# A diffusion block on one core: weight sums spread over another stretch, one sum moved to VectorE, modulation steps two slots earlier, four copies moved to ScalarE

## The chip, the cores and the metric

The kernel runs on one core of a Trainium2 chip. The metric is the device time of one execution in microseconds; the time before is the median of three runs. A trace is one profiled execution, and its times count from the span's start.

## The reference, cut to what matters

One layer works on 512 tokens of 1024 channels (float32), with 256 context tokens as a prefix. Its weights are read once from HBM.

```python
z = h @ w_in                                  # h: x, normed and modulated by c
u, vs, q, r, ga, gb, k, v, lr = split(z)
a  = spatial_gating(gelu(u), gelu(vs), ...)   # 128-token chunks
o  = gla_bidir(q, k, v, lr, ...)              # 4 heads, decays, two directions
ob = rms_norm(o) * gla_norm_g * silu(r)
merged = sigmoid(ga) * (a @ w_br_a) + sigmoid(gb) * (ob @ w_br_b)
x = x + g1 * (merged @ w_o)
x = x + g2 * conv_ffn(modulate(rms_norm(x), sh2, sc2))   # w_up, 3x3 conv, gelu, w_down
out = rms_norm(x)
# sh1, sc1, g1, sh2, sc2, g2 = split(silu(c) @ w_ada + b_ada)
```

## The kernel before, in words

Every product is made nearly exact in float32 by splitting both operands into a high and a low part (float32r) and adding three matmuls: high x high, high x low, low x high. TensorE (PE) does 4440 matmuls, most of them 128x128 by 512.

**The weight stream.** All weights but the very first come as a list of 190 loads of up to 512 KB (`specs`). `weights()` hands out the next one, splits one load further (`stream_split`) and issues loads up to four further (`stream_load`, L240, on SyncE's queue). A load fills one of five buffers `raw`; ScalarE casts it to the high part `wh` (L255), VectorE subtracts to get the low part `wl` (L256), and then the buffer is free for the load five places on. Loads are named here by their place in the list: 18 to 31 belong to r, 32 to 45 to vs, 46 to 59 to ga, 60 to 73 to gb, 74 to 87 to br_a. Loads 10 to 17 are the eight units of u.

**The gates.** r, vs, ga, gb and br_a are each a 1024-wide product of 512 tokens, made in seven products where eight quarters would be needed (`gate`, `gate_product`, a Strassen scheme). One product takes two loads and 24 matmuls into two PSUM banks (L1358). Some products go on accumulating in a bank whose earlier content has to be copied out first: r's fifth (s3) runs on in bank X, out of which ScalarE copies u2 (`taken`, L1341). The scheme needs sums and differences of quarters of the weight. They are built in DRAM ahead of time by GpSimd's DMA queue (POOL): plain copies (L221) and accumulating DMAs (L223), each 512 KB, in `sums_build`. A gate takes 16 of these (8 copies, 8 accumulating), or 12 (6 and 6) when it is one of the first `ADDED` gates: then the first sum is not built, the quarter itself is loaded, and VectorE adds to it the load two places before (`back`, L251). Held by that add, the older buffer comes free later.

**When the sums are issued.** `gate_sums` yields after every sum, and three callers take the next one. `weights()` takes one at each load before r, and from r on where `gate_pace` says so. `hook()`, called after the products of the first stages (each unit of u calls it twice), takes one more at every call from load 8 on. Some places in the first products take one directly. A sum is tied behind the last matmul issued before it (`behind_pe`).

**Heads.** The four heads of the linear attention run in `steps`, fed by `hook`, between the big products. `step_o` writes a head's output to four PSUM banks, two after two; each is copied to SBUF by VectorE (L1020), and ScalarE makes its sum of squares (L1022). Only then is the bank free; the next head's transposes (L953) take these banks.

**Modulation.** g1, sh2 and sc2 are computed on VectorE in small steps beside the gates (`ada2`): one step loads 256 KB of `w_ada` (L1184, SyncE) and does one multiply-add of 128x512 (L1188). A new group first fills its accumulators on ScalarE (L1174) and loads a row of `b_ada` into each (L1176, SyncE). `tick` takes one step; `ticks` is a list of how many steps are taken at each load of a gate.

**gb and the operand of br_a.** After gb's first product SyncE issues 16 loads of a kept operand (`aq<-kept`, L1501, in `a_prep`), which br_a will use. Where the code does not tie an order, a scheduler sets it for each engine.

Of the kernel before, what the change touches and what calls it, by code (L numbers as in the profile page):

```python
# [38 lines left out]
SHSC = 6  # L39
WT = (1, 1)  # L40
RAW = 5
ADDED = 3


@with_exitstack
def backbone_kernel(
# [7 lines left out]
    V, A, G, T = nc.vector, nc.scalar, nc.gpsimd, nc.tensor  # L54
# [19 lines left out]
    def late(shape, dt=F32, s="l"):  # L74
        return lp.tile(shape, dt, tag="l", name=nm(s))
# [7 lines left out]
    def gl():  # L83
        return pg.tile([P, 512], F32, tag="gl", name=nm("gl"))
# [81 lines left out]
    R_AT = len(specs)  # L166
# [14 lines left out]
    def w_block(ap, kn=2, back=0):  # L181
        specs.append((ap.rearrange("(k p) c -> p k c", p=P), kn, 512, back))
# [9 lines left out]
    for g, (g_quarter, g_sums) in enumerate(gate_weights):  # L192
        for n, f in enumerate((lambda b: g_quarter(b, 0, 0),
                               lambda b: g_quarter(b, 0, 1) if g < ADDED else g_sums[b][0], lambda b: g_sums[b][1],
                               lambda b: g_quarter(b, 1, 0), lambda b: g_sums[b][3], lambda b: g_quarter(b, 1, 1),
                               lambda b: g_sums[b][2])):
            for b in range(2):
                w_block(f(b), back=2 if n == 1 and g < ADDED else 0)
    down_specs[R_AT:R_AT] = specs
# [13 lines left out]
    def sums_build(quarter, sums, added=False):  # L213
        for step in ((((1, (0, 0)), (2, (1, 0)), (3, (0, 1))), ((3, (1, 1)),), ((1, 3),), ((2, 1),)) if added else
                     (((0, (0, 1)), (1, (1, 1)), (2, (1, 0)), (3, (0, 1))), ((0, (0, 0)), (3, (1, 1))),
                      ((1, 0),), ((2, 1),))):
            for b in range(len(sums)):
                for dst, src in step:
                    ap = quarter(b, *src) if isinstance(src, tuple) else sums[b][src]
                    if len(step) > 2:  # L220
                        behind_pe(lambda: G.dma_start(sums[b][dst], ap), G)  # L221
                    else:
                        behind_pe(lambda: G.dma_start(sums[b][dst], ap, accum_op=ALU.add), G)  # L223
                    yield

    def gate_sums():
        for g, z in enumerate(gate_weights):
            yield from sums_build(*z, g < ADDED)

# [3 lines left out]
    pos = [0, 0, 0]  # L233
# [37 lines left out]
        return lambda: V.tensor_tensor(wl, raw, wh.bitcast(F32), op=ALU.subtract)  # L271

    def gate_pace(i):
        return i % 3 if i > 45 else i % 4 == 0

    def weights():
        i = pos[2]
        pos[2] += 1
        for at, steps_ in building:
            for _ in range((i >= at and (at > 1 or i < R_AT or gate_pace(i))) + (at <= i < DENSE)):  # L280
                next(steps_, None)
        stream_split(i + 2)
        stream_load(i + 1 + AHEAD)
        return splits.pop(i)
# [648 lines left out]
    def mm3(ps, a, b, start, stop):  # L933
        for z, (p_, q_) in enumerate(((a[0], b[0]), (a[0], b[1]), (a[1], b[0]))):
            T.matmul(ps, p_, q_, start=(start and z == 0), stop=(stop and z == 2))  # L935
# [75 lines left out]
    def step_o(h, part):  # L1011
        S_ = heads[h]
        for i in ((1, 2), (0, 3))[part]:
            po = gl()
            oc = po[:, :256]
            for d in range(2):
                mm3(oc, [z[:, i * P:(i + 1) * P] for z in S_["qs"][d]], S_["st"][d][i], d == 0, False)
            mm3(oc, [z[:, i * P:(i + 1) * P] for z in S_["pt"]], S_["v"][i],
                False, True)
            V.tensor_copy(S_["o"][i // 2][:, i % 2, :], oc)  # L1020
            junk = late([P, 256], BF16, s="junk")
            A.activation(junk, oc, AF.Square, accum_out=oss[:, h, i:i + 1])  # L1022
        if part == 1:
            S_.clear()
# [3 lines left out]
    hooked = [0]  # L1028

    def hook():  # L1030
        hooked[0] += 1
        if (hooked[0] % 2 or pos[2] >= 8) and pos[2] < R_AT:
            next(building[1][1], None)
        if hooks:
            f = hooks.pop(0)
            f[0](*f[1:])
# [4 lines left out]
    def ctx_k(h, part):  # L1041
        ps = mm()
        for k in range(KT):
            wh, wl = part(k)
            ah, al = hc[k]
            for i, (a, b) in enumerate(((wh, ah), (wh, al), (wl, ah))):
                T.matmul(ps[:, :LC], a, b, start=(k == 0 and i == 0), stop=(k == KT - 1 and i == 2))  # L1047
        kcs[h] = heap([P, LC], s="kc")
        A.copy(kcs[h], ps[:, :LC])
        hook()  # L1050
# [5 lines left out]
    def x_unit(store, h):  # L1056
        w = weights()
        ps = mm()
        prod_cm(ps, w, hx)
        store[h] = heap([P, S], s="kq")  # L1060
        if store is qxs:
            A.mul(store[h], ps, QS)
        else:
            V.tensor_copy(store[h], ps)
        hook()
        return lambda k: [z[:, k, :] for z in w]

    def v_units():

        ws = [weights() for _ in range(KT // 2)]  # L1070
        v = []
        for t in range(6):
            ps = mm()
            for k in range(KT):
                wide_step(ps, ws[k // 2], hx if t < 4 else hc, t % 4, k)
            v.append(split_act(ps, s="v", lo_pool=late if t < 3 else heap, hi_pool=late, eng=A.copy))
            for h in (2, 3):
                heads[h].setdefault("v", []).append([z[:, (h - 2) * 256:(h - 1) * 256] for z in v[t]])
            hook()
            hook()  # L1080

    def steps(h):
        if h + 1 < NH:
            rest = [(step_u, h, 0, 3), (step_z, h + 1), (lambda: None,)]
        else:
            rest = [(step_u, h, n, n + 1) for n in range(3)]
        return [(step_transpose, h), (step_scores, h), (step_s0, h)] + rest + [(step_o, h, 0), (step_o, h, 1)]
# [275 lines left out]
    def gate(out, pool, at={}, mids=late, quad=r_quad, sum_=r_sum, pool1=None):  # L1363
        pool1 = pool1 or pool

        fresh = not banks
        banks.extend([bank() for _ in range(2)] for bank in (mm, gl, mm) if fresh)
        X, Z, Y = banks
        banks.reverse()
        later = lambda i: at.get(i, lambda: None)()  # L1370
        gate_product(X, quad("a11"), True)
        if fresh:
            m1 = [taken(z, mids) for z in X]
        else:
            for t in range(2):
                A.copy(Y[t], X[t])
        later(0)
        gate_product(Z, sum_("p1"), True)
        m5 = [taken(z, mids) for z in Z]
        later(1)  # L1380
        gate_product(X, sum_("s2"))
        u2 = [taken(z, mids) for z in X]
        later(2)
        gate_product(Y, quad("a21"), fresh)
        for t in range(2):
            out(0, t, combine(Y[t], m1[t], ALU.add, pool) if fresh else Y[t])
        later(3)
        gate_product(X, sum_("s3"))
        for t in range(2):
            out(1, t + 2, combine(m5[t], X[t], ALU.subtract, pool1))  # L1390
        later(4)
        gate_product(Z, sum_("q4"))
        for t in range(2):
            out(1, t, combine(Z[t], u2[t], ALU.subtract, pool1))
        later(5)
        gate_product(X, quad("a22"))
        later(6)
        for t in range(2):
            out(0, t + 2, X[t])
# [15 lines left out]
    def r_step(i):  # L1415
        if i == 2:
            piece()
        if i in (3, 5):
            sgu_load(i // 2 - 1)

    bg += [ada2("g1", ahead=5), ada2("sh", "sc", ahead=SHSC)]
    ticks = [0] * 4 + [1, 0] * 5 + [1, 0] * 7 + [0, 0] + [1] * 12 + [0, 1] * 7 + [1, 1, 2] * 5
    gate(r_out, heap, {i: lambda i=i: r_step(i) for i in range(7)}, heap)
    vraw = [[None] * 4 for _ in range(2)]
    stats = const([P, 4, 2, 6], "stats")
# [516 lines left out]
```

## Time and profile before

| what | value |
|---|---|
| time, three runs | 904.29 us median (903.58 to 906.23) |
| profiled execution, own time | 907.04 us |
| its span, first to last instruction | 905.3 us |
| mean granted TensorE clock | 0.996 |
| stage r (loads 18 to 31) | 246.2 to 288.6 us |
| stage vs (32 to 45) | 288.6 to 331.6 us |
| stage ga (46 to 59) | 331.6 to 377.9 us |
| stage gb (60 to 73) | 377.9 to 417.1 us |
| stage br_a (74 to 87) | 417.1 to 455.3 us |

A row of the profile gives engine, line, operation, and what was written from what (`wh<-raw`). A wait is put down to the one whose signal came last. The DMA share is the mean busy share of the core's 16 DMA engines; queue q0 is POOL's, q1 SyncE's, q10 ScalarE's. A share can stand a little over 1, since packets overlap. "Granted clock" is 1.00 when TensorE runs at full speed.

### The profile page before, as it was taken

The numbers are of one execution on the slowest core, as the hardware profiler recorded it, in microseconds if no ns is written. First come the engines' busy times: TensorE is split into PE (matmuls) and PEld (weight loads), VectorE is DVE, ScalarE is ACT, GpSimd is POOL, SyncE is SP. The second block draws the span as 40 slices with busy tenths as digits, with TensorE's granted clock in tenths as the row PEclk, the third lists the DMA queues.
The fourth block names the chain that finished last, engine by engine and source line by source line (L and its number), as shares of the span: only waits on it lengthen the run. The fifth ranks groups of instructions, "written<-read, shape, count | busy, mean of one in ns | idle before, by whom it ended". The sixth has DMA issues, their size and how long they took to land.

```text
span 905.3 us, 12519 instructions
## 1 busy us (share of the span) xinstructions
PE 888.0 (98%) x4440; PEld 739.6 (82%) x4440; DVE 733.9 (81%) x1223; ACT 481.4 (53%) x795; POOL 96.6 (11%) x150
## 2 busy tenths in 40 slices
PE   7999999999999999999999999999999999999996
PEld 5778888888877888888888889888888888888885
DVE  6478687969739889769998658897899987896996
ACT  6356465757636765577432348433343334356663
POOL 1302222222200000000000010001111110000000
PEclk9999999999999999999999999999999999999999
DMA  9976999999999977778995961998998893356552
GB/s 298 360 242 171 247 280 212 195 289 247 315 269 280 342 243 259 261 240 274 368 364 165 292 179 47 280 303 180 189 219 178 176 193 98 92 167 207 173 180 99
DMA packets 160268, 207.66 MB, mean 229 GB/s; under 512 B 9625, under 2 KB 88805, under 8 KB 160205
## 3 DMA queue, kind: packets, MB, share of 16 engines
q1 hardware_dynamic: 132861, 140.53, 48.6%
q0 software_dynamic: 24352, 61.04, 31.0%
q10 hardware_dynamic: 2992, 5.28, 1.5%
q8 instruction: 35, 0.57, 0.2%
q14 instruction: 28, 0.23, 0.1%
HBM read 198.43 MB, written 67.11 MB: 293 GB/s over the span
## 4 chain that ended last, share of the span: by engine, by line
PE 90%; DMA 4%; DVE 2%; ACT 2%; issue 0%; SPq 0%; ACTq 0%
PE mm L399 32%; PE mm L1358 13%; PE mm L417 10%; PE gl L1839 10%; PE gl L1358 5%; PE gl L935 2%; PE mm L699 2%; DMA fq<-fx 2%; DMA raw<-in_w_in_dram 2%; PE mm L1839 2%; PE gl L699 1%; PE mm L1047 1%; PE mm L1097 1%; PE gl L417 1%; PE gl L608 1%; PE gl L970 1%
## 5 line engine op out<-in xcount | busy, mean ns | idle before, releaser
L255 ACT CAST wh<-raw 128x1024 fp32r<-128x1024 f32 x189 | 194.8, 1036 | 189.3 <-PE mm L399 89.0
L256 DVE TENSOR_TENSOR wl<-raw,wh 128x1024 fp32r<-128x1024 f32 x189 | 226.1, 1203 | 61.8 <-ACT wh L255 60.2
L399 PE MATMUL mm<-h2h,wh 128*128 128x512 f32 (+1 forms) x344 | 133.0, 387 | 0.0
L399 PE MATMUL mm<-h2l,wh 128*128 128x512 f32 (+1 forms) x344 | 133.0, 387 | 0.0
L399 PE MATMUL mm<-h2h,wl 128*128 128x512 f32 (+1 forms) x344 | 133.0, 387 | 0.0
L1691 DVE SCALAR_TENSOR_TENSOR cacc<-ca,ccol,cacc 128x441 f32<-128x441 f32 (+2 forms) x176 | 121.9, 695 | 4.4
L399 PEld LDWEIGHTS mm<-h2h,wh 128*128 128x128 f32 x344 | 64.6, 188 | 13.1
L399 PEld LDWEIGHTS mm<-h2h,wl 128*128 128x128 f32 x344 | 64.6, 188 | 13.1
L399 PEld LDWEIGHTS mm<-h2l,wh 128*128 128x128 f32 x344 | 64.6, 188 | 13.0
L1839 PE MATMUL gl<-wh,dah 128*128 128x512 f32 x132 | 51.3, 389 | 0.0
L1839 PE MATMUL gl<-wl,dah 128*128 128x512 f32 x132 | 51.3, 389 | 0.0
L1839 PE MATMUL gl<-wh,dal 128*128 128x512 f32 x132 | 51.3, 389 | 0.0
L221 POOL DMA_DIRECT2D sum<-in_ffn_w_down_dram x24 | 13.2, 554 | 310.2 <-PE mm L417 196.1
L1188 DVE SCALAR_TENSOR_TENSOR acc<-wa,cs,acc 128x512 f32<-128x512 f32 x64 | 46.3, 749 | 0.0
L1692 ACT ACTIVATE cacc<-cacc 128x512 f32<-128x512 f32 x22 | 13.9, 633 | 59.4 <-DVE cacc L1691 59.4
L1358 PE MATMUL mm<-wh,xs 128*128 128x512 f32 x128 | 42.4, 402 | 2.7 <-ACT dt L1341 2.7
L223 POOL DMA_DIRECT2D sum<-sum x32 | 27.8, 869 | 149.0 <-PE mm L399 54.9
L399 PE MATMUL mm<-hxh,wh 128*128 128x512 f32 x104 | 40.9, 393 | 0.0
L399 PE MATMUL mm<-hxl,wh 128*128 128x512 f32 x104 | 40.6, 391 | 0.0
L399 PE MATMUL mm<-hxh,wl 128*128 128x512 f32 x104 | 40.5, 390 | 0.0
L1358 PE MATMUL mm<-wh,hxh 128*128 128x512 f32 x96 | 37.7, 393 | 0.0
L1358 PE MATMUL mm<-wh,hxl 128*128 128x512 f32 x96 | 37.4, 390 | 0.0
(473 smaller groups left out, 2018.0 us busy)
## 6 DMA issues: line engine op xcount, KB each, us to landing
raw<-sum SPq DMA_DIRECT2D x54, 512.0 KB, 4.9
raw<-in_w_in_dram SPq DMA_DIRECT2D x50, 512.0 KB, 9.2
wa<-in_w_ada_dram SPq DMA_DIRECT2D x96, 256.0 KB, 5.3
raw<-in_ffn_w_up_dram SPq DMA_DIRECT2D x44, 512.0 KB, 5.9
sum<-in_w_in_dram POOLq DMA_DIRECT2D x36, 512.0 KB, 8.8
sum<-sum POOLq DMA_DIRECT2D x30, 512.0 KB, 7.9
sum<-in_ffn_w_down_dram POOLq DMA_DIRECT2D x30, 512.0 KB, 7.2
raw<-in_ffn_w_down_dram SPq DMA_DIRECT2D x15, 512.0 KB, 3.7
```

The lines of the kernel that those rows point to most:

```text
L223: behind_pe(lambda: G.dma_start(sums[b][dst], ap, accum_op=ALU.add), G)
L255: A.copy(wh, raw)
L256: V.tensor_tensor(wl, raw, wh.bitcast(F32), op=ALU.subtract)
L399: T.matmul(ps, a[:, k, :], b[:, c0:c0 + n], start=(k == 0 and i == 0), stop=(k == KT - 1 and i == 2))
L417: T.matmul(ps, a[:, t * P:(t + 1) * P], b[:, k % 2, :], start=(k == 0 and i == 0), stop=(k == KT - 1 and i == 2))
L699: T.matmul(fps[i], a, b, start=(k == 0 and z == 0), stop=(k == KT - 1 and z == 2))
L935: T.matmul(ps, p_, q_, start=(start and z == 0), stop=(stop and z == 2))
L1188: behind_last(lambda: V.scalar_tensor_tensor(acc[i], coming.pop(0), cs[:, k, 0:1], acc[i], op0=ALU.mult, op1=ALU.add), V)
L1358: T.matmul(banks[t], a(kk, t), w[:, kk, :], start=(first and b == 0 and kk == 0 and i == 0), stop=(b == 1 and kk == 1 and i == 2), skip_gr ...
L1691: V.scalar_tensor_tensor(o, a_[:, r0 + dy:r1 + dy, c0 + dx:c1 + dx], wcol(tap), o, op0=ALU.mult, op1=ALU.add)
L1692: A.activation(acc, acc, AF.Gelu)
L1839: T.matmul(ps, a, w[:, kk, :], start=(first and kk == 0 and i == 0), stop=(last and kk == n_ - 1 and i == 2), skip_group_check=True)
```

## The change

Four edits.

- `ADDED` goes from 3 to 4, so gb is one of the gates whose first sum VectorE makes: 12 sums in DRAM where there were 16, two more adds of 128x1024 (L251), and loads 62 and 63 come from `w_in` itself.
- The pace of the sums. In u's units `hook` takes a sum at every fourth call where it took one at every call. From r on, `gate_pace` took one at every fourth load (20, 24, 28, 32; then none were left). Now it takes them at 20, 24 and 28, then at odd loads from 51. So by r's first load 53 of now 64 sums have been issued, where it was 64 of 68. Three more, copies, are issued in r. The last eight, all accumulating and all of br_a, are issued at loads 51, 53, ... 65, from ga's third product to gb's third.
- `ticks`: r's first four loads took no step of `ada2`, and every second load from then on did; now every second load does from r's first on. All later steps come two earlier.
- `step_o` of the second head (h == 1) copies its four outputs with ScalarE.

```diff
-ADDED = 3
+ADDED = 4
...
     def gate_pace(i):
-        return i % 3 if i > 45 else i % 4 == 0
+        return i % 4 == 0 if i < R_AT + 14 else i > R_AT + 31 and i % 2
...
-            V.tensor_copy(S_["o"][i // 2][:, i % 2, :], oc)
+            (A.copy if h == 1 else V.tensor_copy)(S_["o"][i // 2][:, i % 2, :], oc)
...
     def hook():
         hooked[0] += 1
-        if (hooked[0] % 2 or pos[2] >= 8) and pos[2] < R_AT:
+        if (hooked[0] % 4 == 0 if pos[2] > R_AT - 8 else hooked[0] % 2 or pos[2] >= 8) and pos[2] < R_AT:
             next(building[1][1], None)
...
-    ticks = [0] * 4 + [1, 0] * 5 + [1, 0] * 7 + [0, 0] + [1] * 12 + [0, 1] * 7 + [1, 1, 2] * 5
+    ticks = [1, 0] * 14 + [0, 0] + [1] * 12 + [0, 1] * 7 + [1, 1, 2] * 5
```

`R_AT` is 18. Three places of the order of instructions follow.

SyncE around gb's start, before: the last loads 62 to 67 (the numbered `sum` tiles 163, 167, 164 and 168 are gb's sums in DRAM) and the first of the 16 loads of br_a's operand.

```order
L240 DMA raw_4131<-sum_163 128x2x512
L240 DMA raw_4141<-sum_167 128x2x512
L240 DMA raw_4175<-sum_164 128x2x512
L240 DMA raw_4181<-sum_168 128x2x512
L240 DMA raw_4237<-in_w_in_dram 128x2x512
L240 DMA raw_4243<-in_w_in_dram 128x2x512
L1501 DMA aq_4209<-kept_4056 128x256
```

The same place after: loads 62 to 66 and the first of the 16; then what follows the last of the 16, from load 67 on.

```order
L240 DMA raw_4127<-in_w_in_dram 128x2x512
L240 DMA raw_4134<-in_w_in_dram 128x2x512
L240 DMA raw_4173<-sum_164 128x2x512
L240 DMA raw_4181<-sum_168 128x2x512
L240 DMA raw_4243<-in_w_in_dram 128x2x512
L1501 DMA aq_4214<-kept_4052 128x256
```

```order
L1501 DMA aq_4235<-kept_3986 128x256
L240 DMA raw_4250<-in_w_in_dram 128x2x512
L1176 DMA acc_4252<-in_b_ada_dram 1x512
L1176 DMA acc_4255<-in_b_ada_dram 1x512
L1176 DMA acc_4258<-in_b_ada_dram 1x512
L1176 DMA acc_4261<-in_b_ada_dram 1x512
L1184 DMA wa_979_4264<-in_w_ada_dram 128x512
L240 DMA raw_4306<-sum_166 128x2x512
```

Loads 62 and 63 read the weight itself; load 67 has moved from ahead of the 16 to behind them, and the four rows of `b_ada` and a load of `w_ada` stand ahead of load 68 (`sum_166`).

VectorE over the end of ga and the start of gb, before (`dc` are ga's last combined outputs, `wl` the splits of loads 60 to 64, `accl` a step of `ada2`), and after.

```order
L1346 TENSOR_TENSOR dc_4117<-gl_2992,dt_3926 128x512
L256 TENSOR_TENSOR wl_4138<-raw_4080,wh_4137 128x1024
L1346 TENSOR_TENSOR dc_4120<-gl_2993,dt_3928 128x512
L256 TENSOR_TENSOR wl_4172<-raw_4087,wh_4171 128x1024
L256 TENSOR_TENSOR wl_4178<-raw_4131,wh_4177 128x1024
L392 TENSOR_TENSOR accl_4134<-acc_3088,acch_4133 128x512
L256 TENSOR_TENSOR wl_4234<-raw_4141,wh_4233 128x1024
L256 TENSOR_TENSOR wl_4240<-raw_4175,wh_4239 128x1024
```

```order
L1346 TENSOR_TENSOR dc_4113<-gl_2981,dt_3917 128x512
L256 TENSOR_TENSOR wl_4131<-raw_4076,wh_4130 128x1024
L1346 TENSOR_TENSOR dc_4116<-gl_2982,dt_3919 128x512
L256 TENSOR_TENSOR wl_4170<-raw_4087,wh_4169 128x1024
L251 TENSOR_TENSOR raw_4127<-raw_4127,raw_4076 128x1024
L256 TENSOR_TENSOR wl_4178<-raw_4127,wh_4177 128x1024
L251 TENSOR_TENSOR raw_4134<-raw_4134,raw_4087 128x1024
L256 TENSOR_TENSOR wl_4240<-raw_4134,wh_4239 128x1024
L256 TENSOR_TENSOR wl_4247<-raw_4173,wh_4246 128x1024
```

The two adds stand between the splits, each ahead of the split of its own load, and the second behind the split of load 62.

ScalarE where the second head ends and the third begins, before (`gl` are the four banks, `wh` the casts of loads 11 and 12, `kT` the third head's transposed keys), and after.

```order
L391 CAST vh_2044<-mm_2019 128x512
L255 CAST wh_2308<-raw_1547 128x1024
L255 CAST wh_2460<-raw_2110 128x1024
L1022 ACTIVATE junk_2060,oss<-gl_2049 128x256
L1022 ACTIVATE junk_2073,oss<-gl_2062 128x256
L1022 ACTIVATE junk_2087,oss<-gl_2076 128x256
L1022 ACTIVATE junk_2100,oss<-gl_2089 128x256
L720 CAST kT_2144<-gl_2140 128x384
```

```order
L391 CAST vh_2044<-mm_2019 128x512
L1020 COPY o_1515<-gl_2049 128x256
L1022 ACTIVATE junk_2060,oss<-gl_2049 128x256
L1020 COPY o_1516<-gl_2062 128x256
L1022 ACTIVATE junk_2073,oss<-gl_2062 128x256
L1020 COPY o_1515<-gl_2076 128x256
L1022 ACTIVATE junk_2087,oss<-gl_2076 128x256
L1020 COPY o_1516<-gl_2089 128x256
L1022 ACTIVATE junk_2100,oss<-gl_2089 128x256
L255 CAST wh_2308<-raw_1547 128x1024
L255 CAST wh_2458<-raw_2110 128x1024
L720 CAST kT_2144<-gl_2140 128x384
```

The four copies and squares now alternate, and stand ahead of the two casts.

## The prediction

> **What bounds the kernel now.** The page comes first, for the share of each engine: TensorE (PE) is busy for 98% of the span, so only the time in which it stands still, or runs at a lower clock, can be won without taking work away.
>
> ```profile
> PE 888.0 (98%) x4440; PEld 739.6 (82%) x4440; DVE 733.9 (81%) x1223; ACT 481.4 (53%) x795; POOL 96.6 (11%) x150
> ```
>
> Next, PE's own waits (total us, times, longest).
>
> ```profile
> PE mm L463 <- DMA rows<-in_b_ada_dram: 5.5, 1, 5.5
> PE mm L1358 <- ACT dt L1341: 2.7, 1, 2.7
> PE gl L953 <- ACT junk L1022: 0.4, 1, 0.4
> ```
>
> The 5.5 us are the first loads, which the diff leaves alone. The 2.7 us lie in the gates (L1358), the 0.4 in the heads. The chain of work that ended last, around the gates' wait, tells its cause (start, length, what).
>
> ```profile
> 239.18 17.21 DMA fq<-fx
> ...
> 256.45 15.39 DMA raw<-in_w_in_dram
> ...
> 271.94 1.04 ACT wh L255
> 272.99 0.49 ACT dt L1341
> ...
> 273.53 1.65 PE mm L1358 x3
> ```
>
> A weight load was under way for 15.39 us. ScalarE, which works in order, stood before that load's cast (L255); behind the cast stood the copy of u2 out of the bank (L1341) into which r's fifth product accumulates on, and PE waited for the copy. So the late load was not even the one that PE needed next. The stage by windows (the edges are starts of products; after the length: busy PE, busy weight loads, granted clock, DMA share, GB/s):
>
> ```profile
> 246.16:267.92 21.76, 21.76 (x97) 18.02 (x96) 1.00 1.09 266
> 267.92:277.70 9.78, 7.05 (x26) 5.40 (x24) 0.83 0.92 293
> 272.95:276.36 3.41, 2.83 (x7) 2.25 (x8) 0.50 0.72 243
> ```
>
> Four undisturbed products take 21.76 us, 5.44 each. The fifth takes 9.78, so 4.34 us are lost: 2.83 us of matmuls ran at half the clock, which costs 1.4, and the other 2.9 are the wait. The Trainium skill (TensorE: Matmul & The Clock Gate, Part 1: The HAM clock gate) has the clock halved only after an idle window of about 3.4 us. The trace differs: 2.7 us of idling did it. By that rule a wait of this length would have cost 1.4 us less; the measured 4.34 stands in the sum.
>
> Why the load was late: DMA queues from 200 to 300 us (packets, MB, share of the 16 engines; then issues with KB and median us to landing), and the same from 340 to 400.
>
> ```profile
> q0 software_dynamic: 5210, 12.01, 56.5%
> q1 hardware_dynamic: 10520, 16.28, 48.1%
> ...
> raw<-in_w_in_dram SPq DMA_DIRECT2D x13, 512.0 KB, 12.3
> sum<-in_w_br_a_dram POOLq DMA_DIRECT2D x12, 512.0 KB, 16.2
> ...
> sum<-sum POOLq DMA_DIRECT2D x8, 512.0 KB, 10.2
> ```
>
> ```profile
> q1 hardware_dynamic: 8043, 13.13, 68.8%
> q10 hardware_dynamic: 1416, 2.57, 11.2%
> ...
> raw<-in_w_in_dram SPq DMA_DIRECT2D x8, 512.0 KB, 3.5
> ```
>
> With the weight sums (q0) the engines are full, 104.6%, and a load lands in 12.3 us; later, at 80% and with no sum, in 3.5.
>
> **The change part by part.** *The sums.* From 278 to 300 us only two accumulating sums run; POOL's timeline and the queue from 276 to 300 price them.
>
> ```profile
> 278.16 0.88 POOL L223 DMA_DIRECT2D sum<-sum  x1 [14.34 <-PE mm L1358]
> 289.06 0.88 POOL L223 DMA_DIRECT2D sum<-sum  x1 [10.02 <-PE mm L1358]
> ```
>
> ```profile
> q0 software_dynamic: 544, 1.05, 26.3%
> ```
>
> 26.3% of 24 us are 6.3, so 3.2 us of all engines for each. The 20 sums between 200 and 300 are by the code 12 that accumulate (38 us) and 8 copies, which get the other 18 of the 56.5. By the new pace 3 that accumulate and the 8 copies of br_a fall there: 28 us. The share drops from 104.6 to 76%, under the 80% at which loads landed in 3.5 us. The load that was late needs to land only some 3 us sooner, so the wait should go with its half clock: **-4.3**. Bounds: 0, if another transfer held it, and 4.34. When it goes, the next thing late in r is nothing that this trace shows.
>
> *gb's first sum on VectorE.* Two sums in DRAM become two adds.
>
> ```profile
> L251 DVE TENSOR_TENSOR raw<-raw,raw x6: 1174/1218/1226, 227.9 to 332.5; 128x1024 f32<-128x1024 f32 x6
> ```
>
> ```profile
> 377.93:383.86 5.93, 5.93 (x28) 4.88 (x26) 2.98 (x3) 3.39 (x5) 0.00 (x0) 1.00 0.93 313
> ```
>
> That is 2.4 us of VectorE, in products where it is busy for 2.98 of 5.93 us (third pair; the first two are PE's): hidden. What isn't hidden is a chain. Loads have five buffers; those of loads 60 and 61 are now held until the adds to 62 and 63. Before (VectorE, SyncE, ScalarE, and the chain's row of gb's third to fifth products):
>
> ```profile
> 373.30 2.35 DVE L256 TENSOR_TENSOR wl<-raw,wh 128x1024 fp32r<-128x1024 f32 x2
> ```
>
> ```profile
> 374.54 1.51 SPq L240 DMA_DIRECT2D raw<-in_w_in_dram  x2
> 376.14 8.49 SPq L1501 DMA_DIRECT2D aq<-kept  x16
> 384.74 0.88 SPq L240 DMA_DIRECT2D raw<-sum  x2
> ```
>
> ```profile
> 390.62 1.05 ACT L255 CAST wh<-raw 128x1024 fp32r<-128x1024 f32 x1 [0.48 <-DMA raw<-sum]
> ```
>
> ```profile
> 389.99 16.37 PE mm L1358 x72
> ```
>
> Split of 61 at 373.3 (1.2 us), add 62 (1.2), cast (1.05), split of 62 (1.2), add 63 (1.2): only at 379.2 is the buffer for load 66 free, which was issued at 374.5. Behind it now stand the 16 aq issues (8.5 us), and load 67 behind those: at about 388 where it was issued by 376. The fourth product starts at 389.99 + 5.44 = 395.4 and wants load 67 six matmuls later, at 396.8. Cast and split take 2.3, so the load may take 6.3 us from issue to landing. Low end: load 68, issued behind the same aq loads at 384.74, was waited for and landed at 390.6, in 5.8 us without sums: nothing is late. High end: the 12.3 us of the sums' stage: 6 us late, 7.4 with the half clock. The eight accumulating sums that moved, all of br_a's, come one to a product from ga's third to gb's third, 3.2 us in every 5.4 to 7; no backlog of them stands as it did when they took 16.2 us to land. I take 7.3 us, near the low end, whose row is of this very place: 1 us late, and no half clock charged for so short a stop: **+1.0**. The Trainium skill (DMA: Bandwidth & Descriptors, Queues, rings and completion order) says that each DMA engine takes turns between queues, a packet from each; that speaks against the change, since the moved sums then take turns from gb's loads as they did from r's, and by it alone the sum would come to the first rival's 904.3. The trace agrees that a queue with sums slows the other, 12.3 against 3.5 us.
>
> br_a's sums themselves are not late: by the code each is issued at least six products, some 33 us, before the load that reads it may go out.
>
> *The second head's copies.* ScalarE, VectorE and PE at the place, and a copy of that form on ScalarE:
>
> ```profile
> 167.53 2.00 ACT L255 CAST wh<-raw 128x1024 fp32r<-128x1024 f32 x2
> 170.50 0.38 ACT L1022 ACTIVATE junk<-gl 128x256 bf16<-128x256 f32 x1 [0.97 <-DVE o L1020]
> ```
>
> ```profile
> 169.98 1.42 DVE L1020 COPY o<-gl 128x256 f32<-128x256 f32 x4
> ```
>
> ```profile
> 171.03 1.21 PE L953 MATMUL gl<-ident,lx 128*128 128x128 f32 x6 [0.45 <-ACT junk L1022]
> ```
>
> ```profile
> L1049 ACT COPY kc<-mm x4: 353/364/407, 86.1 to 176.5; 128x256 f32<-128x256 f32 x4
> ```
>
> PE waited 0.45 us for a bank that frees after copy and square. The products were done by then, since VectorE's copies ran without a wait of their own, only late in its order. ScalarE can now copy from about 167.5, before the two casts, at 0.36 us each, so the banks are free before 171: **-0.4** (bounds -0.45 and 0). The casts move back by the four pairs of copy and square, under 4 us; their weights are used two units of products later. Behind them stand the next head's transposed keys, up to 1 us later than now, which PE needs only after the scores: nothing; 1 us if that cover is gone.
>
> *Modulation two steps earlier.* Prices:
>
> ```profile
> L1188 DVE SCALAR_TENSOR_TENSOR acc<-wa,cs,acc x64: 742/747/765, 287.9 to 722.1; 128x512 f32<-128x512 f32 x64
> ```
>
> ```profile
> L1174 ACT ACTIVATE acc<-ident x8: 617/622/634, 249.6 to 588.6; 128x512 f32<-128x512 f32 x8
> ```
>
> Two loads of 256 KB enter r (as much as one weight load, against 28 us less of sums) and two steps of 0.75 us go from ga's VectorE to r's; nothing. In gb four fills of 0.62 us stand ahead of ScalarE's second bank copy, and the four rows of b_ada that SyncE issues after them ahead of load 68, which goes out at about 390 for a use at 395.4 + 5.4 = 400.8: 8.5 us for landing after cast and split, covered unless landing takes over that.
>
> **The sum.** 907.04 - 4.3 + 1.0 - 0.4 = 903.3 for the profiled execution (span 905.3, 1.7 around it). It lies 2.75 above the median, 904.29. If that is the profile's own cost, the median becomes 900.6; if the timed runs had that much less of the wait, they win only 1, 903.3. A wait on a crowded DMA may well differ between runs (their spread is 903.58 to 906.23), but a cost of the profile is the plainer reading: **901.0**.
>
> **The rivals.** First: the crowd moves to gb. For: 80% plus eight sums in some 56 us (46%) is more than the engines gave. Against: the sums come one by one, so no queue of them builds up. At 9.6 us for load 67 the stop is 3.3 + 1.4, all that was won: 904.3.
> Second, slower: the same place, landing as in the chain's 15.39 us. Load 67 is then 9.1 us late, 10.5 with the clock, against 4.7 won: 910.1. It is slower by over 0.3% (2.7 us, about what a measurement can tell from no change) from a landing of 12.3 us on. Against: that landing was reached with four and more sums queued (they took 16.2 us to land, at 3.2 us of work each), and here each has 5.4 us and more to itself.
> Third, the change does not do what it says: r's loads stay late (the fq loads took 17.21 us themselves, in short rows), or the timed runs hardly had the wait: 903.3 to 904.9.
>
> **How the numbers follow.** Forecast 0.55, of which 0.42 win over 2.7 us; first rival 0.20 (0.04 faster, 0.15 same, 0.01 slower); second 0.09, slower; third 0.16 (0.05, 0.10, 0.01). Together faster 0.51, same 0.38, slower 0.11. The range starts at 898.9, with both waits gone whole and gb at nothing (4.8 won, 899.5) and 0.6 for stops too short for the list of waits, and ends at 904.9, so that it takes in the first and third rivals; above it are the slower case and a few hundredths.
>
> **What would show it.** Right: no wait of PE in r, clock 1.00 in every window from 246 on, loads of w_in landing in under 8 us between 200 and 300; the L953 wait gone; in gb's fourth product a stop of about 1 us behind the cast of load 67, issued right after the 16 aq loads. Wrong: a wait in r still there with fewer sums; a stop in gb of over 3 us with a half clock; VectorE, not a load, as the releaser of a new wait in gb or br_a.

## The result and the profile after

The changed kernel took 909.82 us (median of 14 runs, 904.47 to 912.72), the kernel before 903.60 (median of 14, 902.31 to 906.23) on the same chip. The ratio is 1.0058, with a 95% interval of 1.0041 to 1.0076: 0.6% slower (it is not taken from the medians, whose quotient is 1.0069). 901.0 was predicted, with a range up to 904.9.

The two profiled executions say the opposite: the changed kernel's took 904.47 us (span 902.8), that of before 907.04 (span 905.3). Both are at the edge of their runs: 904.47 is the fastest of the 14, and 907.04 lies above all 14 of before. So the profile after shows the right places, but not the typical size. The mean granted clock of the changed kernel's runs says the same: 0.998 in the three fastest (904.47, 905.10 and 906.35 us), 0.993 to 0.996 in the other eleven.

First r's stage. The edges are those of the first four products and of the fifth; the columns are the length, then busy PE, PEld, DVE, ACT and POOL, granted clock, DMA share, GB/s. Then the DMA queues from 200 to 300 us.

```profile
245.31:267.07 21.76, 21.76 (x97) 18.02 (x96) 14.04 (x19) 15.44 (x24) 1.12 (x2) 1.00 0.76 248
267.07:272.51 5.44, 5.44 (x25) 4.50 (x24) 5.44 (x9) 4.51 (x6) 0.00 (x0) 1.00 0.96 307
```

```profile
q1 hardware_dynamic: 10357, 17.50, 53.4%
q0 software_dynamic: 2245, 6.30, 25.9%
```

The fifth product takes 5.44 us like the others, and the sums' queue has 25.9% where it had 56.5. This step went as predicted in this execution. Next, PE's waits from 0.8 us on.

```profile
PE mm L463 <- DMA rows<-in_b_ada_dram: 5.5, 1, 5.5
PE mm L1358 <- ACT wh L255: 1.2, 1, 1.2
PE mm L1358 <- DVE wl L256: 0.8, 1, 0.8
```

The waits of r (L1341) and of the heads (L953) are in no row of the list any more. Two are new, for the cast and for the split of a weight, both in gb's fourth product. The windows show gb's first three products together, the fourth, and the fifth.

```profile
373.42:389.78 16.36, 16.36 (x73) 13.52 (x72) 5.75 (x6) 9.45 (x15) 2.60 (x3) 1.00 1.07 292
389.78:397.72 7.94, 6.01 (x25) 4.43 (x24) 5.26 (x7) 5.64 (x9) 0.00 (x0) 1.00 1.06 360
397.72:403.61 5.89, 5.74 (x25) 4.43 (x24) 5.89 (x8) 5.78 (x8) 0.00 (x0) 1.00 1.00 359
```

The fourth product takes 7.94 us, 2.5 too many, the fifth 0.45 too many, and the DMA engines are full. SyncE's issues and the chain show load 67.

```profile
372.55 0.37 SPq L240 DMA_DIRECT2D raw<-in_w_in_dram  x1
373.01 11.79 SPq L1501 DMA_DIRECT2D aq<-kept  x16
384.90 0.38 SPq L240 DMA_DIRECT2D raw<-in_w_in_dram  x1
```

```profile
378.44 5.76 DMA aq<-kept
...
384.33 0.57 DVE aq L1516
384.90 6.41 DMA raw<-in_w_in_dram
```

Load 67 goes out at 384.90, behind the 16 operand loads, and needs 6.41 us. The 16 took 11.79 us to issue, where they took 8.49 before. SyncE's waits and the chain have 0.2 us more, for VectorE's first combination of the operand (L1516), which itself had waited for an operand load to land.

### The profile page after: what moved, and what is told of

It is laid out like the page before. It is cut to its first block, busy times and chain, and to the rows that moved or that the text cites. A ratio compares the mean times of both kernels' runs of the same rounds, so it can differ in the third digit from the quotient of the medians.

```text
span 902.8 us, 12505 instructions
## 1 busy us (share of the span) xinstructions
PE 886.7 (98%) x4440; PEld 738.9 (82%) x4440; DVE 733.8 (81%) x1221; ACT 482.3 (53%) x799; POOL 93.9 (10%) x146
## 4 chain that ended last, share of the span: by engine, by line
PE 93%; DMA 2%; DVE 2%; ACT 1%; issue 0%; ACTq 0%; SPq 0%; DVEq 0%
PE mm L399 33%; PE mm L1358 13%; PE mm L417 11%; PE gl L1839 10%; PE gl L1358 5%; PE gl L935 3%; PE mm L699 2%; PE mm L1839 2%; PE gl L699 1%; PE mm L1047 1%; PE mm L1097 1%; PE gl L417 1%; DMA aq<-kept 1%; PE gl L608 1%; PE gl L970 1%; PE gl L1227 1%
## 5 line engine op out<-in xcount | busy, mean ns | idle before, releaser
L255 ACT CAST wh<-raw 128x1024 fp32r<-128x1024 f32 x189 | 194.9, 1038 | 185.7 <-PE mm L399 90.3
L1358 PE MATMUL mm<-wl,hxh 128*128 128x512 f32 x96 | 37.5, 391 | 0.8 <-DVE wl L256 0.8
```

The costliest lines, as they stand in the source:

```text
L255: A.copy(wh, raw)
L1358: T.matmul(banks[t], a(kk, t), w[:, kk, :], start=(first and b == 0 and kk == 0 and i == 0), stop=(b == 1 and kk == 1 and i == 2), skip_gr ...
```

## The experiments

Ratios are to the kernel before, run on the same chip (medians there 904.38, 904.17 and 904.67 us in three groups of four), with 95% intervals. The loss sits in gb, at load 67; the theories differ in what makes it late. A: its place behind the 16 operand loads and the moved sums, both needed. B: the place alone. C: the moved sums alone, wherever the load stands. Their rivals came up on the way and stand with the runs that test them.

**gb's first sum by VectorE, alone.**

```diff
-ADDED = 3
+ADDED = 4
```

> The kernel before with ADDED = 4 alone: gb's first sum is made by VectorE, loads 66 and 67 stand behind the 16 loads of br_a's operand, but no sum is moved into ga and gb. Theory A (late place in SyncE's queue and moved sums together): load 67 lands in 4 to 6 us since no sum is in the queues, a stop in gb's fourth product of 1 us at most, 902.5 to 905 us beside 903.6 for the kernel before. Theory B (the place in the queue alone): a stop as in the changed kernel, 907 us or more. Theory C (the moved sums alone): nothing in gb, 902.5 to 904.5 us.

905.2 us, 0.9998 (0.9976 to 1.0021): nothing. In its profile loads 66 and 67 go out behind the 16, at 381.32 and 381.81, and their casts start 6.1 and 7.0 us later, over 2 us before PE needs them. The late place alone does no harm.

**The new pace alone.**

```diff
-        return i % 3 if i > 45 else i % 4 == 0
+        return i % 4 == 0 if i < R_AT + 14 else i > R_AT + 31 and i % 2
...
-        if (hooked[0] % 2 or pos[2] >= 8) and pos[2] < R_AT:
+        if (hooked[0] % 4 == 0 if pos[2] > R_AT - 8 else hooked[0] % 2 or pos[2] >= 8) and pos[2] < R_AT:
```

> The kernel before with the new pace of the sums alone (ADDED stays 3, so there are four more of them, and twelve instead of eight fall in ga, gb and the first load of br_a's stage nearby). Load 67 stands ahead of the 16 operand loads again. Theory A and theory B: no stop in gb's fourth product, r's wait gone, 901 to 903 us. Theory C (the sums crowd the queues wherever the loads stand): late loads in gb, 907 us or more.

910.75 us, 1.0063 (1.0043 to 1.0084): the whole loss, with load 67 ahead of the 16. Theories A and B fail, C stands, though the dose is larger: with `ADDED` at 3 twelve sums come late instead of eight. SyncE's issues, then ScalarE's casts of the operand (L1507) and of load 67 (L255):

```profile
373.84 17.84 SPq L1501 DMA_DIRECT2D aq<-kept  x16
```

```profile
392.26 0.62 ACT L1507 CAST ah<-aq 128x512 fp32r<-128x512 f32 x1 [2.84 <-DVE aq L1516]
392.78 1.05 ACT L255 CAST wh<-raw 128x1024 fp32r<-128x1024 f32 x1
```

```profile
373.38 11.94 DMA raw<-in_w_in_dram
```

By the chain (last row) load 67 had landed at 385.3 here, but its cast stood on ScalarE behind that of an operand tile which waited for a late operand load; the 16 needed 17.84 us to issue. PE's wait there is one of several short ones in gb, none over 0.9 us. The window of its last four products:

```profile
393.02:420.08 27.06, 23.60 (x98) 17.70 (x97) 19.15 (x25) 19.24 (x29) 3.52 (x4) 1.00 1.08 322
```

Four products at full pace take 21.76 us, so 5.3 us are lost here, and the clock stays at 1.00: this loss has no half clock in it. The victims are others, the cause looks the same: what SyncE's queue carries comes late.

**The changed kernel once more.** No edit.

> The changed kernel unaltered, profiled once more to see an execution nearer to its median of 909.8 us than the one at 904.5. All theories put the missing 5 us at one place or another: A and B at gb's fourth product, with a stop of 4 us or more and a granted clock of 0.5 behind it; the other possibility is a stop in a stage that the fast execution does not show at all, br_a or later.

909.3 us, 1.0039 (1.0018 to 1.0061). Its profiled execution took 909.75, close to the median. PE's waits; then the windows of the first three products of gb, of the fourth, and, within that, of the stop and of what follows it; then load 67 in the chain; then one row of what SyncE's queue waited for between 370 and 392 us.

```profile
PE mm L1358 <- ACT wh L255: 3.6, 1, 3.6
PE mm L1358 <- DVE wl L256: 0.8, 1, 0.8
```

```profile
373.85:390.22 16.37, 16.37 (x74) 13.52 (x72) 5.75 (x6) 9.46 (x15) 2.60 (x3) 1.00 1.08 290
390.22:403.46 13.24, 8.86 (x26) 6.47 (x25) 8.12 (x10) 6.93 (x10) 0.00 (x0) 0.74 0.97 323
391.60:395.36 3.76, 0.14 (x1) 0.00 (x0) 0.02 (x1) 1.09 (x2) 0.00 (x0) 1.00 0.97 339
395.36:403.46 8.10, 7.34 (x19) 5.54 (x20) 8.10 (x10) 5.84 (x9) 0.00 (x0) 0.58 0.95 331
```

```profile
385.39 8.79 DMA raw<-in_w_in_dram
```

```profile
SPq L1501 <- DMA aq<-kept: 2.8, 3, 1.9
```

The fourth product takes 13.24 us, 7.8 too many. Everything ahead of it is as in the first profile: the first three products take 16.37 us, and load 67 goes out 11.54 us after gb's start (11.48 there). Only its landing differs, 8.79 us beside 6.41. That makes a stop of 3.76 us out of one so short that the clock stayed at 1.00, and behind it 8.10 us at a mean clock of 0.58, which with 7.34 us busy is some 3.1 us more. So 2.4 us of landing cost 5.3 us of this product's time, and this one place holds the difference between the two profiled spans, 902.8 and 908.0 us.

**The operand loads one product later.**

```diff
     def gb_step(i):
-        a_step((4, 2, 2, 2, 2, 2, 2)[i])
+        a_step((0, 4, 2, 2, 2, 2, 2)[i])
...
     def bra_step(i):
-        a_step((2, 0, 0, 0, 0, 0, 0)[i])
+        a_step((4, 0, 0, 0, 0, 0, 0)[i])
```

> The changed kernel with the 16 loads of br_a's operand issued after gb's second product, so that loads 66 and 67 stand ahead of them. Moved sums, VectorE's adds, modulation and copies stay as changed. Theory A and theory B: the stop in gb's fourth product goes and nothing takes its place, 900.5 to 903 us. Theory C: as changed, 907 us or more. If the stop only moves to loads 68 and 69, which now stand behind the 16: 905 to 910 us, and the list of waits shows it one product later.

909.06 us, 1.0036 (1.0016 to 1.0056), the last of the outcomes named. Loads 66 and 67 are early now, and load 68 takes their place (SyncE, then the chain):

```profile
385.01 10.59 SPq L1501 DMA_DIRECT2D aq<-kept  x13
395.72 0.88 SPq L240 DMA_DIRECT2D raw<-sum  x2
```

```profile
395.72 3.66 DMA raw<-sum
...
399.45 1.05 ACT wh L255
```

PE waits 3.9 us one product later (its list of waits has 3.9 for L255). Load 68 itself lands in 3.66 us; what is late is its issue, behind operand loads, two of which the chain has under way for 7.55 and 7.67 us. Reordering the queue only chose another load to be late.

**The sums beside vs.**

```diff
-        return i % 4 == 0 if i < R_AT + 14 else i > R_AT + 31 and i % 2
+        return i % 4 == 0 if i < R_AT + 14 else i > R_AT + 14 and i % 2
```

> The changed kernel with one number changed: br_a's eight accumulating sums are issued at loads 33, 35, ... 47, beside vs, where it issued them at loads 51 to 65, beside ga and gb. Load 67 stays behind the 16 operand loads. Theory C, as the runs so far leave it (the moved sums fill the DMA engines beside ga and gb, so whatever stands behind the 16 operand loads lands late): no stop in gb, load 67 lands in about 6 us as it did without sums there, and r stays undisturbed: 901 to 902.5 us, the first of these kernels below the kernel before. Rival (sums cost a stop wherever they run): a stop of 3 us or more in vs or ga, 905 us or more. Rival (load 67's place alone, theory B): 907 us or more.

909.13 us, 1.0046 (1.0025 to 1.0068). gb is undisturbed, as theory C had it, but the rival came true: the stop is now in ga.

```profile
PE gl L1227 <- ACT obf L1336: 3.1, 1, 3.1
```

```profile
334.08 9.08 DMA raw<-in_w_in_dram
...
343.23 1.04 ACT wh L255
...
344.66 0.70 ACT obf L1336
```

```profile
341.87:354.96 13.09, 10.04 (x52) 8.45 (x50) 9.71 (x12) 7.45 (x10) 0.00 (x0) 0.87 0.91 292
```

It is r's pattern of before: a late load holds ScalarE at its cast, and behind the cast stands the release of a bank that PE needs (here a head's scaled output, L1336). From the end of the stop, at 345.41, to 349.60 the mean granted clock is 0.59.

**The other three edits, with the old pace.**

```diff
-        return i % 4 == 0 if i < R_AT + 14 else i > R_AT + 31 and i % 2
+        return i % 3 if i > 45 else i % 4 == 0
...
-        if (hooked[0] % 4 == 0 if pos[2] > R_AT - 8 else hooked[0] % 2 or pos[2] >= 8) and pos[2] < R_AT:
+        if (hooked[0] % 2 or pos[2] >= 8) and pos[2] < R_AT:
```

> The changed kernel with the old pace of the sums (hook and gate_pace as before), so the other three edits alone: VectorE makes gb's first sum, modulation two steps earlier, copies on ScalarE. Theory C: no stop in gb; r's stage is as crowded as before and may or may not stop in a given execution: 903 to 904.5 us, within 0.1% of the kernel before. Theory B (load 67's place, with the four rows of the bias behind it): 907 us or more.

905.49 us, 1.0012 (1.0000 to 1.0025), a little over the expected band. gb is undisturbed; r's fifth and seventh products have waits of 0.7 and 0.9 us, with the sums back beside them.

**The copies on ScalarE alone.**

```diff
-            V.tensor_copy(S_["o"][i // 2][:, i % 2, :], oc)
+            (A.copy if h == 1 else V.tensor_copy)(S_["o"][i // 2][:, i % 2, :], oc)
```

> The kernel before with the second head's four copies on ScalarE alone. The wait of PE at the transposes of the next head (0.45 us) goes: 0.4 us less, which may be too small to tell from nothing. Rival: the casts behind the copies come late and cost PE what it won, no difference or 0.3 us more.

905.07 us, 1.0003 (0.9985 to 1.0021). The wait at L953 is gone from its profile; in the time it can't be told from nothing.

**The kernel before once more.**

> The kernel before unaltered, one more profile. If the wait of 2.7 us in r with its half clock belongs to the one execution that was profiled (its own time was 907.04 beside a median of 903.6), this one shows a wait in r of under 1 us and a time of 903 to 904.5. If the wait is in nearly every execution and the profile itself costs 2.7 us: the same wait, and 906 to 907.

903.47 us, and no wait in r at all (the first two rows of PE's list, of which the other three are 0.3 us and less and not in the gates; windows of r's first four products and the fifth; the queues from 200 to 300 us):

```profile
PE mm L463 <- DMA rows<-in_b_ada_dram: 6.1, 1, 6.1
PE gl L953 <- ACT junk L1022: 0.4, 1, 0.4
```

```profile
247.28:269.04 21.76, 21.76 (x97) 18.02 (x96) 12.87 (x16) 14.47 (x23) 1.76 (x2) 1.00 1.08 288
269.04:274.48 5.44, 5.44 (x25) 4.51 (x24) 5.44 (x11) 5.04 (x6) 0.00 (x0) 1.00 1.02 320
```

```profile
q0 software_dynamic: 5186, 11.96, 57.3%
q1 hardware_dynamic: 10214, 16.67, 48.6%
...
raw<-in_w_in_dram SPq DMA_DIRECT2D x14, 512.0 KB, 10.5
```

The engines are as full as in the first profile (105.9%, there 104.6), and loads land in 10.5 us instead of 12.3. This time that was enough. This execution of before without a stop in r takes 903.47 us, and the medians are 903.60 to 904.67. Of the six profiles with the old pace (before twice, gb's first sum alone, the other three edits, the copies, modulation alone) the first is the only one with a stop of over 1 us in r; two of the others (the other three edits, the copies) have short ones of 0.5 to 0.9 us there, three have none.

**The eight sums left out.** br_a is computed with unfinished sums of its weight.

```diff
-        return i % 4 == 0 if i < R_AT + 14 else i > R_AT + 31 and i % 2
+        return i % 4 == 0 if i < R_AT + 14 else False
```

> The changed kernel without the eight accumulating sums that it moved beside ga and gb; they are left out altogether, so br_a is computed with unfinished sums of its weight and the output is incomplete. All else, load 67 behind the 16 operand loads included, is as changed. If those eight sums are the whole cause: no stop in gb, 901 to 902 us, 8 us below the changed kernel. If the place of load 67 has a part of its own: 903 to 906 us.

902.66 us, 0.9980 (0.9967 to 0.9994): beside the changed kernel's 1.0039 and 1.0058 that is 5 to 7 us less. No wait in any gate. SyncE, then ScalarE's cast of load 67:

```profile
373.73 8.68 SPq L1501 DMA_DIRECT2D aq<-kept  x16
382.51 0.38 SPq L240 DMA_DIRECT2D raw<-in_w_in_dram  x1
```

```profile
387.19 1.05 ACT L255 CAST wh<-raw 128x1024 fp32r<-128x1024 f32 x1 [2.85 <-DMA raw<-in_w_in_dram]
```

Load 67 is in the same place of the queue, but goes out 8.4 us after gb's start (374.13) instead of 11.5, lands in 4.7 us and is split 2.4 us ahead of need. So the eight sums are the cause, in two ways: they stretch the issue of the 16 by 3 us, since SyncE waits there for earlier operand loads to land (2.7 and 2.8 us in the two profiles of the changed kernel, no row here), and they stretch load 67 itself.

**The eight sums two products earlier.**

```diff
-        return i % 4 == 0 if i < R_AT + 14 else i > R_AT + 31 and i % 2
+        return i % 4 == 0 if i < R_AT + 14 else i > R_AT + 27 and i < R_AT + 45 and i % 2
```

> The changed kernel with the same eight sums issued two products earlier, at loads 47 to 61, so that the last ones have landed when load 67 goes out at about 385 us. Theory O (the overlap: only the sums under way while load 67 has its 6.3 us do harm): no stop in gb, none in ga, 901 to 903 us. Theory D (the debt: eight sums are about 26 us of all DMA engines, and a stretch in which loads and kept tensors already take most of them cannot give that anywhere from vs to gb; each late load leaves the next ones later): a stop of 2 us or more in ga or early in gb, 905 to 909 us.

904.76 us, 1.0005 (0.9993 to 1.0017), between what the two theories gave. By the ratios 3 to 5 of the 5 to 7 us come back. The 16 still take 12.07 us to issue, beside the last two sums, and load 67 lands in 4.4; what is left are short stops at full clock, in gb's fourth and fifth products.

```profile
390.84:397.01 6.17, 5.75 (x25) 4.43 (x24) 4.43 (x6) 4.68 (x8) 0.00 (x0) 1.00 0.90 312
397.01:403.83 6.82, 6.04 (x26) 4.35 (x25) 6.82 (x9) 6.43 (x9) 0.00 (x0) 1.00 1.01 355
```

gb takes 40.24 us, beside 38.13 without the eight sums. Of the two theories neither holds whole: the overlap with load 67's landing and the half clock behind it are the larger part (O); the overlap with the 16 is the likely rest, which no run here separates. A debt that costs a long stop wherever it is paid (D) would have given one here.

**Modulation alone.**

```diff
-    ticks = [0] * 4 + [1, 0] * 5 + [1, 0] * 7 + [0, 0] + [1] * 12 + [0, 1] * 7 + [1, 1, 2] * 5
+    ticks = [1, 0] * 14 + [0, 0] + [1] * 12 + [0, 1] * 7 + [1, 1, 2] * 5
```

> The kernel before with the modulation steps two earlier alone. Two loads of 256 KB enter r's crowded stage. No difference if they find room (904 to 904.5 us); up to 1 us more, since r's stops, where an execution has them, get longer (905 us).

905.26 us, 0.9998 (0.9973 to 1.0023): nothing.

**The last eight sums spread over r and vs.** This is the kernel before with `ADDED = 4`, the copies on ScalarE, and

```diff
-        return i % 3 if i > 45 else i % 4 == 0
+        return i % 4 == 0
...
-        if (hooked[0] % 2 or pos[2] >= 8) and pos[2] < R_AT:
+        if (hooked[0] % 2 or 8 <= pos[2] <= R_AT - 8) and pos[2] < R_AT:
```

> An attempt at a kernel better than both: gb's first sum by VectorE, copies on ScalarE, old modulation, and the last eight sums (again br_a's) issued at every fourth load from r's third to vs's end (20, 24, ... 48), one in two products. By theory D the debt is paid in small parts from 246 to 331 us, where the loads still have 5 to 9 us of slack: no stop in r, vs, ga or gb, 902 to 903 us, 0.1 to 0.2% below the kernel before. If a stop turns up in vs or ga: 905 us or more.

902.87 us, 0.9975 (0.9959 to 0.9990): 0.25% below the kernel before, and by the ratios 0.6 to 0.8% below the changed one. Its profile has no wait of PE in any gate; the stages r, vs, ga and gb by windows:

```profile
246.68:284.76 38.08, 38.08 (x170) 31.53 (x169) 29.88 (x42) 25.86 (x36) 2.64 (x3) 1.00 0.94 258
284.76:327.40 42.64, 42.64 (x205) 35.41 (x204) 34.92 (x52) 26.94 (x35) 3.50 (x4) 1.00 1.03 311
327.40:373.76 46.36, 46.36 (x243) 39.59 (x242) 43.98 (x61) 28.26 (x37) 0.00 (x0) 1.00 0.71 235
373.76:412.91 39.15, 39.15 (x174) 32.30 (x172) 29.63 (x36) 29.81 (x44) 0.00 (x0) 1.00 0.85 275
```

In all four, PE is busy for the whole length. One sum in two products is carried beside vs even at a share of 1.03; one in each product (the sums beside vs) was not.

## Why the prediction was wrong

**r's wait, -4.3: right in the profiled execution, almost nothing in the median.** With fewer sums the wait went, in all profiles with the thinned pace; but with the old pace only one profile of six had it at full size, so it was one execution's late load and not a fixed cost of the crowd. What failed is the step from the profile to the runs. The 2.75 us between them were read so: "a cost of the profile is the plainer reading". The second profile of before, without the wait, took 903.47 us beside medians of 903.6 to 904.67; a profile has no such cost. From r's start to the end of the span a stop-free execution of before takes 901.8 - 247.28 = 654.5 us, and the changed kernel without the eight sums 900.5 - 246.02 = 654.5. What could be won there in the median were the stops of some executions, about 1 us. The third rival named this ("the timed runs hardly had the wait") and got too little weight.

**gb, "no half clock charged for so short a stop: +1.0": the failed step.** The place, the load and the queue were named rightly; the size was 2.95 us in the fastest execution (two products, 2.50 + 0.45) and 7.8 in the one near the median. That is the whole loss there: the span without the eight sums, 900.5 us, and 7.8 make 908.3, and 908.0 was measured. Three numbers were off: when load 67 goes out, when it is wanted, and the clock. The allowance for load 67 was not 6.3 us but 3.9. It went out 11.5 us after gb's start, where the prediction's times give some 10.2: load 66, ahead of the 16 operand loads, went out 0.9 us before gb's start and not 1.3 us after it (at 372.55, right behind the split of load 62, not behind the second add), but the 16 took 11.8 us to issue instead of the 8.5 of the uncrowded trace. And load 67 was wanted 1.0 us sooner, since gb's first two products, which each held two matmuls of modulation before (17.39 us for three products), ran without them (16.36). No time was won by that: with modulation two steps earlier ga takes 47.4 us where it took 46.4. The landing of 7.3 us was a fair middle for 6.41 and 8.79. And a stop of 3.76 us brought the half clock, some 3.1 us more. So a row without sums was used for how long issues take in a stage with sums, while the landing alone was stretched.

**The first and the second rival.** The first ("the crowd moves to gb") has the mechanism; its 904.3 was too low, because it charged 1.4 us for the clock and subtracted a gain that the median doesn't have. The second gave 910.1 for a landing of 15.39 us. The time came out there with a landing of 8.79, and its bound, slower by over 0.3% "from a landing of 12.3 us on", was too high by the same allowance and the same half clock. Against the first it was said that "the sums come one by one, so no queue of them builds up". They landed in 7.4 to 10.3 us and were issued 5.4 to 7.2 us apart, so two were often under way at once; that was no queue of four, and it was enough beside engines at a share of 1.06. The Trainium skill (DMA: Bandwidth & Descriptors, Queues, rings and completion order), with its turns between queues, pointed the right way: load 67 took 4.7 us without the sums and 6.4 to 8.8 beside one.

**The copies, -0.4; modulation and VectorE's adds, nothing.** The wait at L953 went; its 0.4 us is too small for the runs to show. Modulation and the adds cost nothing alone, 0.9998 each. The long stop ended with ScalarE's cast of a late load (L255, 3.6 us), not with VectorE.

**Not settled:** why load 67 lands in 6.4 us in one execution and in 8.8 in another, with the same issues ahead of it to within 0.1 us.

## What to carry to other kernels

Before a stall of one profile is booked as a gain, look whether the median contains it: a second profile of the unchanged kernel would have shown it absent. Where background transfers are moved into another stage, stretch everything that stands in the queues there, the issue times too, and ask for the load with the least slack; here the half clock added 1.4 us to 2.9 us of stop in one place and 3.1 to 4.4 in another. Spread such work thinly over stages whose loads have slack rather than move it as a block.

## What the runs showed of the hardware

- A row of DMA issues is no fixed price: the same 16 loads took 8.68 us to issue without sums beside them, 11.79 in the changed kernel with its eight late sums, and 17.84 with twelve. Most of the difference is time in which SyncE waited for earlier transfers of its own queue to land: 0.5, 3.4 and 8.9 us (with twelve, 6.6 for weight loads and 2.3 for operand loads).
- Waits of up to 1.2 us left the granted clock at 1.00 (the changed kernel's first profile); waits of 2.7 (before), 3.1 (the sums beside vs), 3.6 (the changed kernel again) and 3.9 us (the operand later) were each followed by a lower clock (0.50, 0.59, 0.58 and 0.64 on the mean of the 3.4, 4.2, 8.1 and 9.1 us behind them), which cost 1.4 us after the first and some 3.1 after the third.
- The same program, with the same queue ahead of a load, took 6.41 and 8.79 us for it in two executions, and the kernel's run times spread over 8 us (904.47 to 912.72). The kernel before spread over 4 us in that group, and reached 911.18 and 913.12 in two of the later ones (one execution of 1276.27 us left aside).
